# Normalised rows before the transposes, and eight gate blocks emitted before the first short-convolution blocks

## The chip, the cores and the metric

One NeuronCore of a Trainium2 chip runs the whole program. The metric is the device time of one execution in microseconds (us), lower is better. Engines are called as the profile calls them: PE (TensorE), PEld (its weight loads), DVE (VectorE), ACT (ScalarE), POOL (GpSimd), SP (SyncE, which only issues DMAs here).

## What is computed

One encoder layer on x of 1024 positions x 1024 channels, float32:

```
h    = rms_norm(x, g_norm)
proj = h @ w_in                                  # 1024 x 5280
hy_in, z_hy, c_q, c_kv, k_rope, z_attn, gate_hy, gate_attn = split(proj)
v, x1, x2 = split(short_conv(hy_in))             # 3 taps, 512 channels each
spec = rfft(filters from a small sine network)   # does not depend on x
zc = x2 * long_conv(x1 * long_conv(v, spec0), spec1)
u_hy   = (zc * silu(z_hy)) @ w_hy_out
u_attn = (attention(c_q, c_kv, k_rope) * silu(z_attn)) @ w_attn_out
gates  = sigmoid([gate_hy, gate_attn] + b_gate)  # 1024 x 2048
out    = x + (g_hy * u_hy + g_at * u_attn) @ w_out
```

## The kernel before

Every large product is made of three matmuls: each operand is split into a rounded high part and the rest (`split`, L132 to L134: an ACT copy gives the high part, DVE or POOL subtracts it for the low part; `gsplit`, L136 to L138, does the same with a factor per partition), and high x high, low x high and high x low are summed in PSUM.

The stages, in the order in which the program emits them:

- **hT** (`build_hT`, L195 to L231). The eight 128x1024 row tiles of x are transposed on PE into h with channels on partitions, in two halves of 512 positions. For each half: transposes as the tiles land (L204), squares with row sums on DVE or ACT (L210, L212), 1/sqrt by integer guess and three Newton steps on tiny DVE tiles (`rsqrt`), eight matmuls that spread the four columns of row factors over a 128x512 tile R (L218, L220), then for each of eight channel blocks d a DVE multiplication by g_norm and R out of PSUM into `tm` (L230) and a split into hh[d] and hl[d], the low part on POOL for even d. `columns` (L167) transposes the small vectors into per-partition columns.
- **Filter network** (`filter_mlp`): two layers of sines for all positions, mostly DVE instructions of 128x512 (`sin_layer`, L236 to L248). **Tables** (`filter_tables`) and **spectra** (`filter_spectra`, L314 on): four rounds, each of pk matmuls (L333, L334), DVE products and sums, and eight leaves with pu matmuls (L128).
- **First short-conv blocks** (`proj_vx(0)`): four of the 41 projection blocks. A projection block (`proj_block`, L538) loads 128 columns of w_in in two DMAs on SP (L544), splits them (wh on ACT, wl on DVE), and runs 48 matmuls of 128x512 into two PSUM banks pm (L552): 8 d x 3 products x 2 halves of the positions. Four banks are tagged for pm, so two blocks are open at a time. A short-conv block (`short_block`, L573) then copies pm to SBUF (L580, ACT), takes one tap on ACT (L583) and two on DVE (L584, L585); `to_time` transposes the result back and stores it. These blocks and all others keep their SBUF results in one ring of three tiles, tag `ob`.
- **Long convolutions** (`convs(0)`, `proj_vx(1)`, `convs(1)`): chains of leaves, each with pu and pi matmuls. `xz` makes a short-conv block and a SiLU block beside them. The convolutions' pools reuse memory of the filter pools.
- **Latents** (`fill_c`), **q, k, v** (`qkv`), then z blocks (`fill_z`) and the sixteen **gate blocks** (`fill_g`, L662 to L669): a projection block, two ACT sigmoids of 128x512 straight from PSUM into `ob`, one DMA to DRAM issued by ACT. They have no DVE work but the wl split.
- **Attention**, output projections, tail.

The emission order is a priority, not the order of execution: a planner that knows each instruction's inputs, buffers and an estimate of its duration fixes the order on every engine ahead of time, and lets later-emitted work in wherever earlier-emitted work is not ready. Within an engine the fixed order is then kept.

Of the kernel before, what the change touches and what calls it, by code (L numbers as in the profile page):

```python
# [19 lines left out]
P = 128  # L20
# [12 lines left out]
HSPLIT = 3  # L33
CVB, MMB = 2, 4
# [58 lines left out]
class K:  # L93
# [22 lines left out]
    def mm3(self, out, lh, ll, rh, rl, start, stop, after=None):  # L116
        nc = self.nc
        m = nc.tensor.matmul(out, lhsT=lh, rhs=rh, start=start, stop=False)  # L118
        if after is not None:
            self.tc.add_manual_dep(m.ins, after.ins.name, mybir.DependencyInfo(mybir.DependencyClass.NoSync, mybir.DependencyReason.DATA), reason="slack")  # L120
        nc.tensor.matmul(out, lhsT=ll, rhs=rh, start=False, stop=False)  # L121
        nc.tensor.matmul(out, lhsT=lh, rhs=rl, start=False, stop=stop)  # L122

    def mm6(self, out, terms, after=None):

        ops = [(x, t[2]) for t in terms for x in t[:2]] + [(t[0], t[3]) for t in terms]
        for n, (x, y) in enumerate(ops):
            m = self.nc.tensor.matmul(out, lhsT=x, rhs=y, start=n == 0, stop=n == len(ops) - 1)  # L128
            if n == 0 and after is not None:
                self.tc.add_manual_dep(m.ins, after.ins.name, mybir.DependencyInfo(mybir.DependencyClass.NoSync, mybir.DependencyReason.DATA), reason="slack")  # L130

    def split(self, x, hi, lo, eng=None):  # L132
        self.nc.scalar.copy(out=hi, in_=x)  # L133
        (eng or self.nc.vector).tensor_tensor(out=lo, in0=x, in1=hi.bitcast(F32), op=ALU.subtract)  # L134

    def gsplit(self, x, g, hi, lo):  # L136
        self.nc.scalar.activation(out=hi, in_=x, func=AF.Copy, scale=g)
        self.nc.vector.scalar_tensor_tensor(out=lo, in0=x, scalar=g, in1=hi.bitcast(F32), op0=ALU.mult, op1=ALU.subtract)  # L138

# [16 lines left out]
    def setup(self, xp):  # L156
# [7 lines left out]
        self.selr = xp.tile([P, P], F32, tag="selr", name="selr")  # L164
        nc.scalar.dma_start(out=self.selr, in_=a["sel"])

    def columns(self):  # L167
# [16 lines left out]
        self.sel = cp.tile([P, P], F32R, tag="sel", name="sel")  # L184
        nc.scalar.copy(out=self.sel, in_=self.selr)


    def load_x(self, xp, g):
        self.xt = getattr(self, "xt", [])
        for tt in range(4 * g, 4 * g + 4):  # L190
            x = xp.tile([P, D], F32, tag=f"x{tt}", name=self.nm("x"))
            self.nc.sync.dma_start(out=x, in_=self.a["x"][0, tt * P:(tt + 1) * P, :])
            self.xt.append(x)

    def build_hT(self, hp, xp):  # L195
        nc, a = self.nc, self.a
# [3 lines left out]
        xt = self.xt  # L200
        for g in range(2):
            tags = ("mm", "mm", "mm", "mm", "tp", "tp", "cv") if g == 0 else ("tp", "tp", "cv")
            bank = lambda t: self.pp.tile([P, 512], F32, tag=t, bufs={"mm": MMB, "tp": 2, "cv": CVB}[t], name=self.nm("ptx"))
            tr = lambda d, i: nc.tensor.transpose(out=ps[d][:, i * P:(i + 1) * P], in_=xt[4 * g + i][:, d * P:(d + 1) * P], identity=self.ident)  # L204
            ps = {d: bank(t) for d, t in enumerate(tags)}
            for i in range(4):
# [6 lines left out]
                for d in range(len(tags)):  # L213
                    tr(d, i)
            rs = self.rsqrt(xp, ss[:, 4 * g:4 * g + 4], 1.0 / D, [P, 4], "xr")
            pr = self.pp.tile([P, 4, P], F32, tag="cv", bufs=CVB, name=self.nm("prs"))
            for i in range(4):
                nc.tensor.matmul(pr[:, i], lhsT=rs[:, i:i + 1].broadcast_to([P, P]), rhs=self.ident, start=True, stop=True)  # L218
            R = xp.tile([P, 512], F32, tag="R", name=self.nm("R"))
            nc.scalar.copy(out=R, in_=pr.rearrange("p a b -> p (a b)"))  # L220
            if g == 0:
                self.columns()
            sl = slice(g * 512, (g + 1) * 512)
            for d in range(8):
                if d not in ps:
                    ps[d] = bank(("tp", "cv")[d % 2] if g else "tp")
# [1007 lines left out]
```

## Time and profile before

| | us |
|---|---|
| median of 3 runs (lowest to highest) | 1177.83 (1176.38 to 1181.05) |
| the profiled execution | 1176.94 |
| span in its trace | 1174.9 |
| PE busy in the span | 1111.1 |
| DVE busy in the span | 902.8 |
| ACT busy in the span | 585.0 |

The trace covers one execution from its first to its last instruction; 2.0 us of the execution lie outside the span. Matmuls overlap, so the mean duration of one is longer than the distance between two. The granted clock is that of PE: 1.00 is 2.4 GHz, 0.50 is 1.2 GHz, values between are means over a stretch.

### The profile page before, as it was taken

The numbers are of one execution on the slowest core, as the hardware profiler recorded it, in microseconds if no ns is written. First come the engines' busy times: TensorE is split into PE (matmuls) and PEld (weight loads), VectorE is DVE, ScalarE is ACT, GpSimd is POOL, SyncE is SP. The second block draws the span as 40 slices with busy tenths as digits, with TensorE's granted clock in tenths as the row PEclk, the third lists the DMA queues.
The fourth block names the chain that finished last, engine by engine and source line by source line (L and its number), as shares of the span: only waits on it lengthen the run. The fifth ranks groups of instructions, "written<-read, shape, count | busy, mean of one in ns | idle before, by whom it ended". The sixth has DMA issues, their size and how long they took to land.

```text
span 1174.9 us, 15580 instructions
## 1 busy us (share of the span) xinstructions
PE 1111.1 (95%) x5541; PEld 916.1 (78%) x5541; DVE 902.8 (77%) x1629; ACT 585.0 (50%) x1096; POOL 121.2 (10%) x118
## 2 busy tenths in 40 slices
PE   4979989999999999999999999999999999999996
PEld 3757767788888878888887887788888888777875
DVE  5889988898787776877756991388888888668872
ACT  5546454655443523434425742477777777322320
POOL 3200000000000000000000234100000000132253
PEclk7979989999999999999999999999999999999999
DMA  5344445443234344343338458420202010786335
GB/s 190 94 121 147 137 152 197 157 148 89 86 99 121 121 117 126 95 143 90 90 109 264 143 169 297 144 81 2 99 1 90 1 63 2 249 279 206 88 128 179
DMA packets 119221, 150.27 MB, mean 128 GB/s; under 512 B 8548, under 2 KB 82408, under 8 KB 119144
## 3 DMA queue, kind: packets, MB, share of 16 engines
q1 hardware_dynamic: 107832, 122.88, 34.0%
q10 hardware_dynamic: 11312, 26.42, 6.0%
q8 instruction: 43, 0.70, 0.3%
q14 instruction: 34, 0.28, 0.1%
HBM read 101.81 MB, written 47.45 MB: 127 GB/s over the span
## 4 chain that ended last, share of the span: by engine, by line
PE 72%; DVE 12%; DMA 7%; ACT 5%; issue 2%; POOL 1%; SPq 0%; POOLq 0%; DVEq 0%; ACTq 0%
PE pm L552 32%; PE pu L128 6%; PE pt L886 5%; PE pi L128 4%; PE S L118 2%; PE S L121 2%; PE S L122 2%; PE pmo L118 2%; PE pv L898 2%; PE pmo L121 2%; PE pmo L122 2%; PE pv L899 2%; PE po L121 2%; PE po L118 2%; PE po L122 2%
## 5 line engine op out<-in xcount | busy, mean ns | idle before, releaser
L552 PE MATMUL pm<-hh,wh 128*128 128x512 f32 x656 | 212.2, 397 | 6.7 <-DVE sg L626 3.7
L552 PE MATMUL pm<-hl,wh 128*128 128x512 f32 x656 | 210.1, 395 | 0.5 <-POOL hl L134 0.4
L552 PE MATMUL pm<-hh,wl 128*128 128x512 f32 x656 | 209.2, 394 | 0.5 <-DVE wl L134 0.4
L552 PEld LDWEIGHTS pm<-hh,wh 128*128 128x128 f32 x656 | 124.4, 190 | 35.4 <-DVE sg L626 4.9
L133 ACT CAST wh<-wr 128x512 fp32r<-128x512 f32 x98 | 60.5, 620 | 172.5 <-PE pm L552 139.7
L552 PEld LDWEIGHTS pm<-hh,wl 128*128 128x128 f32 x656 | 123.8, 189 | 27.1 <-DVE wl L134 2.1
L552 PEld LDWEIGHTS pm<-hl,wh 128*128 128x128 f32 x656 | 123.9, 190 | 26.6 <-POOL hl L134 1.2
L134 DVE TENSOR_TENSOR wl<-wr,wh 128x512 fp32r<-128x512 f32 x95 | 71.1, 751 | 43.4 <-ACT wh L133 43.0
L134 DVE TENSOR_TENSOR PTl<-pt,PTh 128x512 fp32r<-128x512 f32 x128 | 84.0, 682 | 14.0 <-ACT PTh L133 13.7
L133 ACT CAST PTh<-pt 128x512 fp32r<-128x512 f32 x128 | 72.8, 587 | 43.3 <-PE pt L886 41.5
L871 DVE TENSOR_REDUCE mx<-S 128x1 f32<-128x1024 f32 x64 | 77.8, 1218 | 10.5 <-PE S L122 10.3
L886 PE MATMUL pt<-ident,pr 128*128 128x128 f32 x512 | 75.1, 276 | 1.1 <-ACT pr L873 0.2
L873 ACT ACTIVATE pr<-S,mx 128x1024 f32<-128x1024 f32 x64 | 71.7, 1121 | 5.7 <-DVE mx L871 5.1
L886 PEld LDWEIGHTS pt<-ident,pr 128*128 128x128 f32 x512 | 59.0, 140 | 15.5 <-ACT pr L873 2.9
L898 PE MATMUL pv<-PTh,vc 128*128 128x256 f32 x256 | 69.0, 297 | 0.0
L458 DVE TENSOR_TENSOR t<-pu,kt 128x512 f32<-128x512 f32 x64 | 41.1, 682 | 35.2 <-PE pu L128 34.3
L899 PE MATMUL pv<-PTl,vc 128*128 128x256 f32 x256 | 67.8, 293 | 0.0
L133 ACT CAST rh<-res 128x512 fp32r<-128x512 f32 x64 | 39.3, 618 | 41.8 <-DVE res L366 17.2
L118 PE MATMUL S<-kh,qh 96*128 96x512 f32 x128 | 53.0, 414 | 1.7 <-ACT pr L873 1.6
L121 PE MATMUL S<-kh,ql 96*128 96x512 f32 x128 | 52.5, 410 | 0.0
L898 PEld LDWEIGHTS pv<-PTh,vc 128*128 128x128 f32 x256 | 48.6, 190 | 4.4 <-DVE at L909 1.6
L799 POOL TENSOR_TENSOR k<-k,ry 128x512 f32<-128x512 f32 x8 | 11.6, 1452 | 380.8 <-DVE rv L146 377.4
(289 smaller groups left out, 2469.6 us busy)
## 6 DMA issues: line engine op xcount, KB each, us to landing
wr<-in_w_in_dram SPq DMA_DIRECT2D x82, 256.0 KB, 3.2
wor<-in_w_out_dram SPq DMA_DIRECT2D x36, 256.0 KB, 4.8
dec<-in_dec_dram SPq DMA_DIRECT2D x16, 512.0 KB, 4.2
gT<-ob ACTq DMA_DIRECT2D x16, 512.0 KB, 3.2
gg<-gT SPq DMA_DIRECT2D x16, 512.0 KB, 4.5
kd<-kt ACTq DMA_DIRECT2D x28, 256.0 KB, 2.4
kt<-kd SPq DMA_DIRECT2D x28, 256.0 KB, 2.7
x<-in_x_dram SPq DMA_DIRECT2D x8, 512.0 KB, 6.1
```

The costliest lines, as they stand in the source:

```text
L118: m = nc.tensor.matmul(out, lhsT=lh, rhs=rh, start=start, stop=False)
L121: nc.tensor.matmul(out, lhsT=ll, rhs=rh, start=False, stop=False)
L122: nc.tensor.matmul(out, lhsT=lh, rhs=rl, start=False, stop=stop)
L128: m = self.nc.tensor.matmul(out, lhsT=x, rhs=y, start=n == 0, stop=n == len(ops) - 1)
L133: self.nc.scalar.copy(out=hi, in_=x)
L134: (eng or self.nc.vector).tensor_tensor(out=lo, in0=x, in1=hi.bitcast(F32), op=ALU.subtract)
L552: nc.tensor.matmul(ps[c][0:m], lhsT=w[:, i, 0:m], rhs=h[d][:, c * 512:(c + 1) * 512], start=(d == 0 and f == 0), stop=(d == 7 and f == 2))
L871: nc.vector.tensor_reduce(out=mx, in_=ps, axis=AX.X, op=ALU.max, negate=True)
L873: nc.scalar.activation(out=pr, in_=ps, func=AF.Exp, bias=mx, accum_out=RS[h // 2][:, qb, h % 2:h % 2 + 1])
L886: nc.tensor.transpose(out=pt[:, i], in_=pr[:, kb * P:(kb + 1) * P], identity=self.ident)
L898: nc.tensor.matmul(pv, lhsT=V[h][:, kb], rhs=hi[:, kb], start=(kb == 0), stop=False)
L899: nc.tensor.matmul(pv, lhsT=V[h][:, kb], rhs=lo[:, kb], start=False, stop=(kb == 7))
```

## The change

Rows of x are multiplied by their own factor before they are transposed (tiles xs, DVE), so that squares and factors come first and the eight spreading matmuls, R and `tm` go; g_norm goes into the split, which reads PSUM on both engines. POOL has no part in hT or in z2 any more. The x tiles are issued by SP and ACT in turn, all eight ahead of the filter's loads, and those go to SP. The filter network's first splits are ordered behind the last split of hT's first half on ACT, the cast of `sel` behind the network. The weight tiles wh and wl get four buffers each. Eight of the sixteen gate blocks are emitted behind the filter spectra, ahead of `proj_vx(0)`.

```diff
@@ constants
+GEARLY = 8
...
@@ class K
-    def split(self, x, hi, lo, eng=None):
-        self.nc.scalar.copy(out=hi, in_=x)
+    def behind(self, i, after):
...
+    def split(self, x, hi, lo, eng=None, after=None):
+        self.behind(self.nc.scalar.copy(out=hi, in_=x), after)
         (eng or self.nc.vector).tensor_tensor(out=lo, in0=x, in1=hi.bitcast(F32), op=ALU.subtract)
...
@@ def load_x
-            self.nc.sync.dma_start(out=x, in_=self.a["x"][0, tt * P:(tt + 1) * P, :])
+            (self.nc.sync, self.nc.scalar)[tt % 2].dma_start(out=x, in_=self.a["x"][0, tt * P:(tt + 1) * P, :])
@@ def build_hT
-            ps = {d: bank(t) for d, t in enumerate(tags)}
             for i in range(4):
                 tt = 4 * g + i
...
-                for d in range(len(tags)):
-                    tr(d, i)
-            rs = self.rsqrt(xp, ss[:, 4 * g:4 * g + 4], 1.0 / D, [P, 4], "xr")
-            pr = self.pp.tile([P, 4, P], F32, tag="cv", bufs=CVB, name=self.nm("prs"))
-            for i in range(4):
-                nc.tensor.matmul(pr[:, i], lhsT=rs[:, i:i + 1].broadcast_to([P, P]), rhs=self.ident, start=True, stop=True)
-            R = xp.tile([P, 512], F32, tag="R", name=self.nm("R"))
-            nc.scalar.copy(out=R, in_=pr.rearrange("p a b -> p (a b)"))
             if g == 0:
                 self.columns()
+            rs = self.rsqrt(xp, ss[:, 4 * g:4 * g + 4], 1.0 / D, [P, 4], f"xr{g}")
+            xs = []
+            for i in range(4):
+                x = xp.tile([P, D], F32, tag="xs", bufs=4, name=self.nm("xs"))
+                nc.vector.tensor_scalar(out=x, in0=xt[4 * g + i], scalar1=rs[:, i:i + 1], scalar2=None, op0=ALU.mult)
+                xs.append(x)
...
+            def tr(d, i):
+                nc.tensor.transpose(out=ps[d][:, i * P:(i + 1) * P], in_=xs[i][:, d * P:(d + 1) * P], identity=self.ident)
+
+            n = 7 if g == 0 else 2
+            for d in range(n):
+                ps[d] = bank(tags[d])
+            for i in range(4):
+                for d in range(n):
+                    tr(d, i)
             for d in range(8):
                 if d not in ps:
...
-                t = xp.tile([P, 512], F32, tag="tm", bufs=3, name=self.nm("tm"))
-                nc.vector.scalar_tensor_tensor(out=t, in0=ps[d], scalar=self.gn[:, d:d + 1], in1=R, op0=ALU.mult, op1=ALU.mult)
-                self.split(t, self.hh[d][:, sl], self.hl[d][:, sl], (nc.gpsimd, nc.vector)[d % 2])
+                i = self.gsplit(ps[d], self.gn[:, d:d + 1], self.hh[d][:, sl], self.hl[d][:, sl])
+            self.half0 = getattr(self, "half0", i)
@@ def filter_loads, filter_mlp
+        self.selr = f1.tile([P, P], F32, tag="selr", name="selr")
+        nc.sync.dma_start(out=self.selr, in_=a["sel"])
...
-        nc.scalar.dma_start(out=self.wf1, in_=a["wf1"])
+        nc.sync.dma_start(out=self.wf1, in_=a["wf1"])
...
-        self.split(self.wf1, w1h, w1l)
-        self.split(self.wf2, w2h, w2l)
+        self.split(self.wf1, w1h, w1l, after=self.half0)
+        self.split(self.wf2, w2h, w2l, after=self.half0)
...
-            self.split(z2[:, sl], zh[:, sl], zl[:, sl], nc.gpsimd)
+            self.split(z2[:, sl], zh[:, sl], zl[:, sl], after=self.half0)
@@ def proj_block (the same in proj_rope for wh)
-            wh = wp.tile([P, 4, P], F32R, tag="wh", bufs=3, name=self.nm("wh"))
-            wl = wp.tile([P, 4, P], F32R, tag="wl", bufs=3, name=self.nm("wl"))
+            wh = wp.tile([P, 4, P], F32R, tag="wh", bufs=4, name=self.nm("wh"))
+            wl = wp.tile([P, 4, P], F32R, tag="wl", bufs=4, name=self.nm("wl"))
@@ def hyena_mla_kernel
-                    k.load_x(xp, 0)
                     k.setup(xp)
+                    k.load_x(xp, 0)
+                    k.load_x(xp, 1)
                     k.filter_loads(f1)
-                    k.load_x(xp, 1)
                     k.build_hT(hp, xp)
                     k.filter_mlp(fp, f1)
+                    k.selection()
...
                     with k.pool("fwk") as wk:
                         k.filter_spectra(wk)
+                        for b in range(GEARLY):
+                            k.fill_g(b)
...
-            for b in range(16):
+            for b in range(GEARLY, 16):
                 k.fill_g(b)
```

## Rows read from the trace of the kernel before

**Rows 1.** Page, busy time of each engine (share) and instructions.

```profile
PE 1111.1 (95%) x5541; PEld 916.1 (78%) x5541; DVE 902.8 (77%) x1629; ACT 585.0 (50%) x1096; POOL 121.2 (10%) x118
```

**Rows 2.** Windows, all engines: stretch, its us, busy (instructions) each, PEclk, DMA share, GB/s.

```profile
0.00:25.00 25.00, 9.18 (x41) 7.72 (x41) 11.76 (x27) 12.61 (x25) 7.60 (x12) 0.75 0.64 223
25.00:50.00 25.00, 23.43 (x105) 17.90 (x106) 22.01 (x42) 12.17 (x20) 8.40 (x6) 0.90 0.28 76
50.00:75.00 25.00, 16.46 (x67) 13.03 (x67) 23.69 (x36) 16.19 (x24) 0.13 (x2) 0.78 0.16 47
75.00:100.00 25.00, 25.00 (x127) 21.30 (x126) 21.54 (x37) 10.03 (x18) 0.13 (x2) 0.95 0.68 200
100.00:150.00 50.00, 47.92 (x227) 37.33 (x227) 45.83 (x92) 29.60 (x66) 0.27 (x4) 1.00 0.46 150
150.00:200.00 50.00, 42.64 (x197) 34.60 (x196) 42.42 (x81) 26.51 (x53) 0.13 (x2) 0.90 0.49 158
200.00:250.00 50.00, 48.42 (x228) 39.22 (x227) 45.10 (x82) 29.28 (x58) 0.27 (x4) 1.00 0.52 177
250.00:400.00 150.00, 150.00 (x695) 124.41 (x694) 123.56 (x239) 69.04 (x135) 0.53 (x8) 1.00 0.35 102
400.00:600.00 200.00, 200.00 (x915) 163.67 (x915) 144.12 (x295) 77.99 (x159) 0.00 (x0) 1.00 0.37 110
...
700.00:750.00 50.00, 47.02 (x202) 37.70 (x201) 12.23 (x13) 15.97 (x25) 17.13 (x11) 0.97 0.73 250
```

**Rows 3.** Waits of PE: who waited for whom, us in total, times, longest.

```profile
PE pk L333 <- DVE h L291: 6.5, 1, 6.5
...
PE pu L128 <- ACT rh L133: 4.8, 1, 4.8
```

**Rows 4.** Line L669, the stores of the gate blocks: first and last start.

```profile
L669 ACTq DMA_DIRECT2D gT<-ob x16: 321/326/397, 501.1 to 748.8; - x16
```

**Rows 5.** Timeline, 10 to 28 us: start, us, what, idle before and its releaser.

```profile
10.53 1.23 DVE L210 SCALAR_TENSOR_TENSOR sq<-x 128x1024 f32<-128x1024 f32 x1 [0.48 <-DMA x<-in_x_dram]
...
12.38 2.49 POOL L134 TENSOR_TENSOR zl<-z,zh 128x512 fp32r<-128x512 f32 x2 [9.63 <-ACT zh L133]
12.49 1.18 DVE L150 TENSOR_TENSOR rt<-ry 128x4 f32<-128x4 f32 x1
...
16.10 0.16 DVE L152 SCALAR_TENSOR_TENSOR ry<-rt,ry 128x4 f32<-128x4 f32 x1
...
20.27 1.11 PE L204 MATMUL ptx<-ident,x 128*128 128x128 f32 x4 [0.73 <-ACT cols L172]
...
25.81 0.78 PE L552 MATMUL pm<-hh,wh 128*128 128x512 f32 x1
```

**Rows 6.** Line L242, a DVE operation with one SBUF input: ns min/median/max.

```profile
L242 DVE TENSOR_SCALAR sk<-sx x4: 411/416/429, 46.7 to 61.6; 128x512 f32<-128x512 f32 x4
```

**Rows 7.** Line L138, the low part with a factor, out of PSUM.

```profile
L138 DVE SCALAR_TENSOR_TENSOR ql<-pth,gq,qh x16: 737/737/747, 752.1 to 963.0; 96x512 fp32r<-96x512 f32 x16
```

**Rows 8.** Windows of L552 alone: stretch, us, PE, PEld busy (x), PEclk, DMA, GB/s.

```profile
0.00:50.00 50.00, 17.26 (x59) 11.74 (x60) 0.83 0.46 149
50.00:80.00 30.00, 16.88 (x62) 12.62 (x62) 0.77 0.30 85
80.00:250.00 170.00, 95.41 (x378) 69.30 (x377) 0.97 0.50 164
```

**Rows 9.** Chain of waits, 300 to 345 us: start, us, piece.

```profile
318.39 23.59 PE pm L552 x104
```

**Rows 10.** Groups of DVE, 75 to 250 us: count, busy us, mean ns, idle before.

```profile
L134 DVE TENSOR_TENSOR wl<-wr,wh 128x512 fp32r<-128x512 f32 x16 | 10.9, 678 | 1.8 <-ACT wh L133 1.8
L584 DVE SCALAR_TENSOR_TENSOR acc<-sraw,cols,acc 128x1024 f32<-128x1024 f32 x6 | 7.7, 1276 | 2.5 <-issue 2.2 <-ACT acc L583 0.2
```

**Rows 11.** Line L248, sines on ACT and their table load.

```profile
L248 ACT ACTIVATE sx<-sx x4: 623/630/632, 52.2 to 70.8; 128x512 f32<-128x512 f32 x4
L248 ACT ACT_TABLE_LOAD  x1: 1283/1283/1283, 49.3 to 49.3; - x1
```

More of the change, by code (lines that the diff above doesn't have):

```diff
@@ L118, in mm3 @@
         m = nc.tensor.matmul(out, lhsT=lh, rhs=rh, start=start, stop=False)
-        if after is not None:
-            self.tc.add_manual_dep(m.ins, after.ins.name, mybir.DependencyInfo(mybir.DependencyClass.NoSync, mybir.DependencyReason.DATA), reason="slack")
+        self.behind(m, after)
         nc.tensor.matmul(out, lhsT=ll, rhs=rh, start=False, stop=False)
@@ L128, in mm6 @@
             m = self.nc.tensor.matmul(out, lhsT=x, rhs=y, start=n == 0, stop=n == len(ops) - 1)
-            if n == 0 and after is not None:
-                self.tc.add_manual_dep(m.ins, after.ins.name, mybir.DependencyInfo(mybir.DependencyClass.NoSync, mybir.DependencyReason.DATA), reason="slack")
-    def split(self, x, hi, lo, eng=None):
-        self.nc.scalar.copy(out=hi, in_=x)
+            if n == 0:
+                self.behind(m, after)
+    def behind(self, i, after):
+        if after is not None:
+            self.tc.add_manual_dep(i.ins, after.ins.name, mybir.DependencyInfo(mybir.DependencyClass.NoSync, mybir.DependencyReason.DATA), reason="order")
+    def split(self, x, hi, lo, eng=None, after=None):
+        self.behind(self.nc.scalar.copy(out=hi, in_=x), after)
         (eng or self.nc.vector).tensor_tensor(out=lo, in0=x, in1=hi.bitcast(F32), op=ALU.subtract)
     def gsplit(self, x, g, hi, lo):
-        self.nc.scalar.activation(out=hi, in_=x, func=AF.Copy, scale=g)
+        i = self.nc.scalar.activation(out=hi, in_=x, func=AF.Copy, scale=g)
         self.nc.vector.scalar_tensor_tensor(out=lo, in0=x, scalar=g, in1=hi.bitcast(F32), op0=ALU.mult, op1=ALU.subtract)
+        return i
     def rsqrt(self, pool, ss, inv_n, shape, tag):
@@ L183, in columns, with selection @@
         self.ssc = cp.tile([P, 2, 8], F32, tag="ssc", name="ssc")
-        self.sel = cp.tile([P, P], F32R, tag="sel", name="sel")
-        nc.scalar.copy(out=self.sel, in_=self.selr)
+    def selection(self):
+        self.sel = self.cp.tile([P, P], F32R, tag="sel", name="sel")
+        self.nc.scalar.copy(out=self.sel, in_=self.selr)
     def load_x(self, xp, g):
@@ L200, in build_hT @@
         xt = self.xt
+        bank = lambda t: self.pp.tile([P, 512], F32, tag=t, bufs={"mm": MMB, "tp": 2, "cv": CVB}[t], name=self.nm("ptx"))
         for g in range(2):
-            tags = ("mm", "mm", "mm", "mm", "tp", "tp", "cv") if g == 0 else ("tp", "tp", "cv")
-            bank = lambda t: self.pp.tile([P, 512], F32, tag=t, bufs={"mm": MMB, "tp": 2, "cv": CVB}[t], name=self.nm("ptx"))
-            tr = lambda d, i: nc.tensor.transpose(out=ps[d][:, i * P:(i + 1) * P], in_=xt[4 * g + i][:, d * P:(d + 1) * P], identity=self.ident)
-            ps = {d: bank(t) for d, t in enumerate(tags)}
             for i in range(4):
@@ new lines, in build_hT @@
+            sl = slice(g * 512, (g + 1) * 512)
+            tags = ("mm", "mm", "mm", "mm", "tp", "tp", "cv", "tp") if g == 0 else ("tp", "cv") * 4
+            ps = {}
+            def tr(d, i):
[6 more added lines that the diff above has]
+                    tr(d, i)
@@ L562, in proj_rope @@
         nc.sync.dma_start(out=raw, in_=src[:, :, c0:c0 + 32])
[L563 removed]
+        w = wp.tile([P, 8, 64], F32R, tag="wh", bufs=4, name=self.nm("wh"))
         nc.scalar.copy(out=w[:, :, 0:32], in_=raw)
```

11 lines of the change are left out of this document (4 added, 7 removed).

## The prediction

> **What bounds the kernel now.** I read the busy shares first: PE is busy 95% of the span, DVE 77%, ACT 50% [rows 1]. A kernel in that state can gain in two ways: less PE work, or fewer holes in PE. So the next view is the windows [rows 2], read for two things in each stretch, PE's idle time and its granted clock. From 250 to 600 us PE has no hole and the clock stands at 1.00. Before 250 us it has both: 15.8 us idle in the first 25, 8.5 in 50 to 75 at a mean clock of 0.78, 7.4 in 150 to 200 at 0.90. To put both in one unit I count as lost the idle time plus the busy time multiplied by one minus the clock: 13.4 us for 50 to 100 (8.54 + 3.62 + 0 + 1.25) and 15.3 us for 100 to 250 (2.08 + 7.36 + 4.26 + 1.58). This overstates the clock's part where PE waits anyway, so it is a bound.
>
> Then the waits of PE [rows 3] tell what fills these holes. The longest one, 6.5 us, is the first pk matmul behind DVE's last subtraction of the filter network; another, 4.8 us, is a pu matmul behind a split. Such waits belong to the spectra and would be harmless if PE had something else. It has nothing: the projection blocks that the planner lets in there are short-conv blocks, and each needs DVE work (L584, L585, 1.28 us an instruction [rows 10]) before its ring buffers come free, while DVE is busy 23.7 of 25 us in just that stretch [rows 2]. The blocks that need no DVE but for the two wl splits, the gate blocks, all come after 501 us [rows 4].
>
> Last, the reserve at the other end: from 700 to 750 us PE is 94% busy with DVE at 12.2 of 50 [rows 2]. That stretch is left-over projection work that nothing on DVE waits for. Work that PE does earlier shortens it one for one.
>
> **The change part by part.** The sum is made against the profiled execution, 1176.94 us, of which 1174.9 are the span; it lies 0.9 us under the median of 1177.83.
>
> *Start, hT.* Before: the last of the first four x tiles is squared at 10.53 for 1.23 us; the Newton chain ends at 16.26, two of its tiny instructions taking 1.2 us instead of 0.16 while POOL subtracts zl; spreading, copying and the columns go on to 20.3; the first projection matmul starts at 25.81 [rows 5]. By 50 us 59 of them are done [rows 8]. At full pace one takes 23.59 / 104 = 0.227 us [rows 9].
> After: squares end near 11.8 as now. The chain of eleven instructions at about 0.2 us ends at 14.0, since POOL does nothing then (16.2 if the slow ones stay). Four scalings of 128x1024: a DVE instruction with one SBUF input takes 0.416 us for 512 columns [rows 6] and 0.16 at 4 columns, so 0.66 as an estimate on that line; the upper bound is 1.23, the square of the same shape. That gives 16.6 (to 21.1). The last tile's seven transposes follow, four of them taking 1.11 us at the low clock [rows 5], 2 us: 18.6. Then eight splits at DVE's pace of 0.74 [rows 7]; PE can start with the first, at 19.2, and the half is complete at 25. The second half costs DVE 2.2 + 2.6 + 8 x 0.74, about 37 with its transposes. In the first half two blocks can run on half of their columns, 48 matmuls, until about 38; the remaining 12 us to 50 give 53 more. That is 101 against 59; less 6 small matmuls of the network and some waiting for wl I take 30 more: 30 x 0.227 = 7 us. Bounds: 12 us if nothing waits; with both upper bounds above (16.2, then 1.23 each) hT would be finished near 46, as now, and DVE, which takes over POOL's share, would be later by some 4: so -4.
> Edits that cost nothing: x on two queues (four issues of L192 move from SP to ACT, ahead of z2 and the small loads; 223 GB/s pass in the first 25 us [rows 2], and I take the landing of the first four tiles as unchanged), three small loads leaving ACT's queue for SP's against four x issues coming, the cast of sel. Cover: ACT has 25 us of 50 free there [rows 2]. If the four issues were not hidden, each would put off the first ACT square, some 2 us in all.
>
> *50 to 100 us.* The gate blocks need wl, 2 x 0.68 us of DVE [rows 10], for 10.9 us of PE (48 x 0.227). With them PE runs while DVE makes the sines. They free the ring through ACT and a store alone. Bounds 0 (wl waits behind all of the network) and 13.4. DVE leaves small holes between dependent instructions, into which a planner can put wl, and four buffers allow a block more of lead: I take 9.
> Each gate store is issued by ACT in its own order and waits for the sigmoid before it; behind it stand the casts rh of the spectra. 0.33 us each [rows 4], eight times, moved rather than added.
> Sines and sigmoids now fall into one stretch. There is one table load of 1.28 us ahead of all four sines [rows 11]; interleaved, each sine could need one and each sigmoid after it another: at most 8 x 1.28 = 10 us of ACT, half of them on the network's chain. PE's gate work hides them; without that cover 5 us. The Trainium skill (ScalarE: Activation LUTs, section What ACT_TABLE_LOAD costs) sets a switch at 2.66 us with the drain it adds, and advises finishing one set before the next; by that the chain would be later by an estimated 11 us instead of 5, and the forecast would lose the part of it that is not covered. No row here shows the drain.
>
> *100 to 250 us.* The spectra are bound by DVE (85 to 92% [rows 2]). About half of the short-conv blocks that run here now go later, each taking 2 x 1.28 us of DVE along; eight gate blocks (87 us of PE) come instead. Bounds 0 and 15.3. What the planner's estimates miss stays as holes, so I take 9.
>
> *Later.* The displaced short-conv blocks, about five, bring 13 us of DVE work into 250 to 600, where DVE has 82 us free of 350 [rows 2]: hidden, at a price of 0 to 6 us if it lies on the convolutions' chain; I take 2. The first convolution needs four short-conv blocks, which now come after eight others; PE has work meanwhile. What is late there is covered by the left-over stretch, of which some 40 us are left at 700 (PE works 47 of the 50 us there, with its edges).
>
> Sum: 7 + 9 + 9 - 2 = 23 us. 1176.9 - 23 = 1154, and 0.9 more for the median: **1155**. Best bounds: 12 + 13.4 + 15.3 = 41 us, 1137. Worst: start -4 and later -6, nothing gained: 1188.
>
> **The rivals.**
> *Half of it.* The gate blocks fill the holes of 50 to 100, but the spectra's holes come from buffers and DMA waits that every filler shares, and the start gains little: 3 + 9 + 3 - 2 = 13 us, 1165. For it: the 4.8 us wait falls at a low-activity moment between two rounds, where pm banks may be full. Against it: with fillers of the same machinery PE has no hole from 250 to 600.
> *The holes only move.* PE is fuller before 250, but the fillers are then short at 600 to 750: PE would stand idle in the q, k, v stage. The stretch after 700 holds some 40 us of pure filler, more than the gain, which speaks against it. Time: 1177.
> *DVE bounds the front.* hT now takes DVE 16 x 0.74 + 8 x (0.66 to 1.23) plus z2's two subtractions, against 16 x 0.74 and half of the subtractions before. If wl of the gate blocks is placed behind the network, PE has two open blocks (22 us of matmuls) between 20 us and the first pk matmul and then nothing, as now, and the spectra start later by DVE's extra 4 us; with hT as late as its upper bound (4 more): 1177.8 + 8 = 1186. It decides where fewer than six wl splits stand ahead of the first pk matmul. For it: DVE is the fullest engine there. Against it: the zl contention goes.
> That the gate blocks are not let in at all is excluded by the order: they are the next projection work in priority, and projection blocks already run in these holes.
>
> **How the numbers follow.** Forecast, 1147 to 1160: 0.56; better than that: 0.06; half: 0.17; holes only move: 0.11; DVE bounds the front: 0.10. A measurement of this kernel can tell about 0.5%, 5.9 us, from no change, so the bounds are 1171.9 and 1183.7. Faster: 0.56 + 0.06 + 0.15 of the half case = 0.77; slower 0.09; the same 0.14. The range leaves out most of the better case and the last two cases' upper parts: 1143 to 1176.
>
> **What would show it.** PE's first projection matmul near 19 us and over 85 of them by 50 us; PE over 97% busy at clock 1.00 from 50 to 100; gate stores beginning near 45 us and eight of them before 200; the first leaf of the convolutions starting earlier than now; POOL with no work before 250; a shorter stretch between the last DVE work of q, k, v and the attention. Wrong: a pk wait of PE on DVE that stays, more than three table loads before 100 us on the chain, or new holes of PE between 250 and 700.

## The result, and the profile after

The changed kernel takes 1157.74 us (median of four runs, 1156.19 to 1159.08) where the kernel before takes 1177.11 (four runs, 1174.64 to 1181.05): a ratio of 0.9832 [0.9801, 0.9863]. It is faster, by 19.4 us (1.7%), and lies in the range, 2.7 us above the forecast of 1155. The profiled execution has a span of 1156.9 us against 1174.9, so 18.0 us are to be found in the trace.

The page's busy times after the change, to be held against [rows 1]:

```profile
PE 1098.8 (95%) x5525; PEld 912.7 (79%) x5525; DVE 894.0 (77%) x1631; ACT 589.2 (51%) x1097; POOL 106.7 (9%) x108
```

The shares are the same; what moved is where PE's holes lie. The windows of all engines after, with the columns of [rows 2]:

```profile
0.00:25.00 25.00, 8.99 (x40) 8.08 (x41) 13.51 (x42) 13.50 (x25) 2.09 (x6) 1.00 0.69 244
25.00:50.00 25.00, 24.05 (x122) 19.01 (x121) 24.82 (x42) 20.86 (x30) 0.00 (x0) 1.00 0.31 84
50.00:75.00 25.00, 18.65 (x84) 15.43 (x83) 20.84 (x36) 10.96 (x16) 0.00 (x0) 0.80 0.53 167
75.00:100.00 25.00, 25.00 (x117) 20.62 (x116) 22.07 (x48) 15.02 (x33) 0.00 (x0) 1.00 0.47 160
100.00:150.00 50.00, 50.00 (x254) 42.03 (x253) 40.81 (x82) 24.07 (x50) 0.14 (x2) 1.00 0.57 182
150.00:200.00 50.00, 50.00 (x246) 41.73 (x245) 43.53 (x90) 27.54 (x59) 0.00 (x0) 1.00 0.48 168
200.00:250.00 50.00, 49.32 (x243) 40.87 (x242) 39.83 (x68) 30.68 (x58) 0.53 (x8) 1.00 0.53 159
...
700.00:750.00 50.00, 41.12 (x195) 33.37 (x194) 17.74 (x33) 20.80 (x33) 18.76 (x13) 0.93 0.73 246
```

With the prediction's own unit (idle time plus busy time times one minus the clock), the first 50 us lose 17.0 us where they lost 22.0 in [rows 2], 50 to 100 lose 10.1 (6.35 + 18.65 x 0.20) where it was 13.4, and 100 to 250 lose 0.7 where it was 15.3. That is 5.0 + 3.3 + 14.6 = 22.9 us gained before 250. The 5.0 is the least sure of them: the clock of the first row is no measurement, since this trace has no clock record before 21.6 us (the one of before has none before 9.3), and the windows print 1.00 where there is none. With the lower level taken for that time, which the pace of the transposes bears out (last section), the first 50 us lose an estimated 20.0 where they lost 23.7, and 3.7 + 3.3 + 14.6 = 21.6 are gained. The last line runs the other way: PE stands idle for 8.9 of the 50 us from 700, where it was 3.0.

The first projection matmuls that the gain consists of, counted in the windows of the projection's line alone (L567, before L552):

```profile
0.00:50.00 50.00, 21.72 (x83) 15.11 (x84) 1.00 0.50 164
50.00:80.00 30.00, 19.71 (x74) 14.68 (x73) 0.83 0.58 184
80.00:250.00 170.00, 112.65 (x458) 84.37 (x457) 1.00 0.51 165
```

Against [rows 8] that is 24, 12 and 80 matmuls more, 116 in all, and at 0.227 us [rows 9] 26.3 us of PE work done ahead at 250 us. The lead is still there at the end of the projections: the last one starts at 720.6, before at 747.4, 26.8 us earlier. But the first score matmul starts at 737.1 against 754.8, only 17.7 earlier, and from there to the end it is 419.8 us against 420.1. So about 9 us are lost between the last projection and the first score. The waits of PE say where:

```profile
PE pth L857 <- ACT ob L683: 7.1, 1, 7.1
...
PE pk L348 <- DVE h L306: 5.9, 1, 5.9
```

The second of them is the wait of [rows 3], still there. The first is new. The timeline of ACT around it shows what ACT did meanwhile:

```profile
719.69 1.05 ACT L138 CAST yh<-yr 128x1024 fp32r<-128x1024 f32 x1 [8.47 <-DMA yr<-yT]
721.04 1.04 ACT L138 CAST yh<-yr 128x1024 fp32r<-128x1024 f32 x1 [0.30 <-DMA yr<-yT]
722.31 1.04 ACT L138 CAST yh<-yr 128x1024 fp32r<-128x1024 f32 x1 [0.23 <-DMA yr<-yT]
723.26 1.21 ACT L138 CAST wh<-wr 128x512 fp32r<-128x512 f32 x2
726.47 1.04 ACT L138 CAST yh<-yr 128x1024 fp32r<-128x1024 f32 x1 [2.00 <-DMA yr<-yT]
727.42 1.26 ACT L683 ACTIVATE ob<-pm,cols 128x512 f32<-128x512 f32 x2
```

The last gate sigmoid (L683) frees the PSUM banks that the transposes of q and k (pth) need. Its projection ended at 721.0, but in ACT's order it stands behind four casts of the convolution's output, and each of these waits for its load. The timeline of SP's DMA queue shows when the loads were issued:

```profile
705.53 0.36 SPq L818 DMA_DIRECT2D qd<-q  x1
...
710.00 1.68 SPq L991 DMA_DIRECT2D yr<-yT  x3
...
723.20 0.34 SPq L991 DMA_DIRECT2D yr<-yT  x1
```

The first loads are issued behind the last stores of q and k, at 710.0, and before the change they were issued at 710.5: that end did not move. The data were not what they waited for, since the last store of yT starts at 618.4; issuing the loads earlier was not tried. Before, the same sigmoid started at 747.55, at once after its last projection, because the casts had long been done (the last yh at 725.30). The convolution chain ends where it did (the last pi matmul starts at 595.4, before at 596.8; the last pkv matmul at 686.6, before at 682.3); PE's own work now ends 27 us earlier, ahead of what q, k, v and the loads behind them deliver.

### The profile page after: what moved, and what is told of

Read it like the earlier page. It is cut to its first block, busy times and chain, and to the rows that moved or that the text cites. A ratio compares the mean times of both kernels' runs of the same rounds, so it can differ in the third digit from the quotient of the medians.

```text
span 1156.9 us, 15518 instructions
## 1 busy us (share of the span) xinstructions
PE 1098.8 (95%) x5525; PEld 912.7 (79%) x5525; DVE 894.0 (77%) x1631; ACT 589.2 (51%) x1097; POOL 106.7 (9%) x108
## 4 chain that ended last, share of the span: by engine, by line
PE 77%; DVE 8%; DMA 8%; ACT 4%; issue 2%; POOL 1%; SPq 0%; POOLq 0%; ACTq 0%; DVEq 0%
PE pm L567 35%; PE pu L128 8%; PE pt L901 5%; PE pi L128 4%; PE S L119 2%; PE S L121 2%; PE S L122 2%; PE pv L913 2%; PE pv L914 2%; PE po L122 2%; PE po L121 2%; PE po L119 2%; PE pmo L121 1%; PE pmo L119 1%; ACT pr L888 1%
## 5 line engine op out<-in xcount | busy, mean ns | idle before, releaser
L567 PE MATMUL pm<-hh,wh 128*128 128x512 f32 x656 | 208.8, 394 | 1.4 <-DVE hl L143 0.5
L567 PE MATMUL pm<-hl,wh 128*128 128x512 f32 x656 | 209.4, 394 | 0.0
L567 PE MATMUL pm<-hh,wl 128*128 128x512 f32 x656 | 208.3, 392 | 0.1
L567 PEld LDWEIGHTS pm<-hh,wh 128*128 128x128 f32 x656 | 123.1, 189 | 27.3 <-ACT wh L138 0.7
L567 PEld LDWEIGHTS pm<-hh,wl 128*128 128x128 f32 x656 | 123.4, 189 | 26.0 <-DVE wl L139 0.5
L567 PEld LDWEIGHTS pm<-hl,wh 128*128 128x128 f32 x656 | 123.5, 189 | 25.4
L138 ACT CAST wh<-wr 128x512 fp32r<-128x512 f32 x98 | 60.3, 621 | 152.0 <-PE pm L567 106.9
L138 ACT CAST PTh<-pt 128x512 fp32r<-128x512 f32 x128 | 72.8, 587 | 43.6 <-PE pt L901 41.8
L886 DVE TENSOR_REDUCE mx<-S 128x1 f32<-128x1024 f32 x64 | 77.8, 1218 | 10.5 <-PE S L122 10.1
L139 DVE TENSOR_TENSOR wl<-wr,wh 128x512 fp32r<-128x512 f32 x95 | 66.2, 702 | 16.2 <-ACT wh L138 16.1
L138 ACT CAST rh<-res 128x512 fp32r<-128x512 f32 x64 | 39.5, 619 | 42.8 <-PE pu L128 20.2
L122 PE MATMUL S<-kl,qh 96*128 96x512 f32 x128 | 50.8, 398 | 0.0
```

The lines of the kernel that those rows point to most:

```text
L138: self.behind(self.nc.scalar.copy(out=hi, in_=x), after)
L567: nc.tensor.matmul(ps[c][0:m], lhsT=w[:, i, 0:m], rhs=h[d][:, c * 512:(c + 1) * 512], start=(d == 0 and f == 0), stop=(d == 7 and f == 2))
L886: nc.vector.tensor_reduce(out=mx, in_=ps, axis=AX.X, op=ALU.max, negate=True)
```

## The experiments

Two ends have to meet before attention: PE's queue of projections, and the chain from the first convolution through q, k and v to the casts yh. The theory was that new hT and gate blocks each give a part of the gain and add up, that the wait at 728 is worth its 7 us, and that the hole at 53 us comes from wl on DVE. Each of these three was tried. Ratios are against the kernel before on the same chip, whose medians lie between 1174.8 and 1177.1.

**Without the early gate blocks.**

```diff
-GEARLY = 8
+GEARLY = 0
```

> The changed kernel with no gate block ahead of the first short-conv blocks (all sixteen after the z blocks again); the new hT and all else stay. Theory: the start keeps its 5 us (some 24 more projection matmuls by 50 us), and the holes of PE between 50 and 250 us come back, since the short-conv blocks wait for DVE: 1168 to 1174 us, about 0.993 to 0.997 of the kernel before, PE idle 15 us or more from 50 to 250. Rival (the new hT and the free POOL carry the gain, the gate blocks only move holes): 1160 us, 0.986.

Measured: 1164.9 us, 0.992 [0.9904, 0.9937], better than the theory and short of the rival. The holes do come back: PE is idle for 16.6 us from 50 to 250, with the gate blocks for 7.0. The change without the early blocks, which is the new hT with the edits around it (the order of the splits, the loads, four weight buffers), is worth half of the gain. Below it is called the new hT; of these edits the queues of x and the splits of z2 were tried by themselves, the buffers and the rest were not. The convolutions start earlier than in the changed kernel (first pu matmul of a convolution at 234.7 against 236.2), the last projection starts at 734.3.

**The early gate blocks alone, in the kernel before.**

```diff
+GEARLY = 8
...
+                        for b in range(GEARLY):
+                            k.fill_g(b)
...
-            for b in range(16):
+            for b in range(GEARLY, 16):
```

> The kernel before with nothing changed but eight gate blocks emitted ahead of the first short-conv blocks. Theory: the holes from 50 to 250 us close as in the changed kernel, the start is as before: 1160 to 1166 us, 0.985 to 0.990 of the kernel before. Rival (the new hT carries the gain): 1172 us or more.

Measured: 1174.56 us, 1.0002 [0.9991, 1.0013]: nothing, and the theory of two parts that add falls. The windows show that the gate blocks do what they were meant to do between 100 and 250 us (columns as in [rows 2]):

```profile
100.00:150.00 50.00, 48.73 (x232) 40.03 (x231) 38.27 (x80) 26.64 (x58) 0.00 (x0) 1.00 0.48 161
150.00:200.00 50.00, 49.24 (x248) 40.60 (x247) 40.73 (x80) 23.16 (x49) 0.14 (x2) 1.00 0.54 182
200.00:250.00 50.00, 49.84 (x237) 41.12 (x237) 39.06 (x67) 31.70 (x59) 0.40 (x6) 1.00 0.54 171
```

The last projection starts at 734.9, 12.5 us earlier than before. But the first convolution waits for four short-conv blocks that now stand behind eight others: it starts at 251.4 instead of 246.3, 22.2 us after the last pu matmul of the spectra instead of 15.4, and the chain ends later by more (last pi 612.7 instead of 596.8, last pkv 700.9 instead of 682.3). ACT at the other end, in the timeline of the same run:

```profile
736.05 1.04 ACT L134 CAST yh<-yr 128x1024 fp32r<-128x1024 f32 x1 [10.54 <-DMA yr<-yT]
...
742.65 1.04 ACT L134 CAST yh<-yr 128x1024 fp32r<-128x1024 f32 x1 [1.97 <-DMA yr<-yT]
743.60 1.26 ACT L669 ACTIVATE ob<-pm,cols 128x512 f32<-128x512 f32 x2
```

The last sigmoid again stands behind yh, 8.3 us after the last projection's end, and the first score comes at 753.9, 0.9 earlier than before. With the new hT the chain starts some 12 to 15 us earlier, which is the room that the gate blocks use.

**How many early gate blocks.** Four, twelve and six instead of eight, the constant alone; the diff of the first:

```diff
-GEARLY = 8
+GEARLY = 4
```

> The changed kernel with four gate blocks ahead of the first short-conv blocks instead of eight. Theory: attention's first score matmul starts at the later of two ends, that of PE's projection work, and that of the q, k, v stage plus some 50 us (686.6 and 737.1 in the changed kernel, 700.9 and 753.9 with the gate blocks alone, but 677.2 and 742.4 with none ahead, where PE's work ends last). Eight blocks ahead put off the convolutions, so the second ends last; with four the two are near each other: first scores at 732 to 736, the time 1152 to 1156 us, 0.977 to 0.982 of the kernel before. Rival (each block ahead fills PE further, in proportion): half way between none and eight, first scores near 740, 0.987 to 0.989.

> The changed kernel with twelve gate blocks ahead. Theory: the convolutions, and with them the last pkv matmul, come later again, at 691 us or more; first scores at 741 or more, 1160 to 1166 us, 0.985 to 0.990 of the kernel before. Rival (more blocks ahead, fewer holes): first scores at 737 or earlier, not over 1158 us.

> The changed kernel with six gate blocks ahead. Theory (first scores wait for the later of PE's projection work and the q, k, v stage; the first convolution starts when PE has finished the gate blocks ahead and four short-conv blocks, but not before the spectra let it, at 234 us): the first pu matmul of the convolutions stays at 233 to 237 us, the projection work ends near 726, first scores at 732 to 736, the time 1152 to 1156 us, 0.978 to 0.982 of the kernel before. Rival (what four gain at one end they lose at the other, whatever the number between): 0.983 as with four and eight, first scores at 737 or later.

Measured: four 1156.57 us, 0.9831 [0.9809, 0.9852]; twelve 1188.99, 1.0106 [1.0087, 1.0126]; six 1160.63, 0.9877 [0.9859, 0.9894]. Four is as good as eight, six is 0.5% behind them, just clear of the interval of four, and twelve is slower than no change at all. For four and six I had expected 1152 to 1156 us and first scores from 732 to 736: both came out above. Why six is behind four is not shown; the spans of the three traces (1157.9, 1157.7, 1156.9) do not tell them apart. The starts of five steps in the traces, in us, with two runs of below:

| run | first convolution pu | last pi | last pkv | last projection | first score |
|---|---|---|---|---|---|
| before | 246.3 | 596.8 | 682.3 | 747.4 | 754.8 |
| gate blocks alone | 251.4 | 612.7 | 700.9 | 734.9 | 753.9 |
| new hT, none early | 234.7 | 588.4 | 677.2 | 734.3 | 742.4 |
| new hT, four | 233.8 | 585.6 | 674.0 | 730.9 | 739.0 |
| new hT, six | 232.5 | 590.7 | 678.4 | 728.8 | 739.9 |
| the change, eight | 236.2 | 595.4 | 686.6 | 720.6 | 737.1 |
| new hT, twelve | 279.5 | 637.9 | 724.7 | 661.8 | 757.2 |
| casts behind, eight | 234.6 | 594.4 | 683.9 | 717.9 | 729.1 |
| three ahead of the network, six | 254.8 | 609.1 | 696.9 | 721.6 | 741.3 |

Read the last two columns together. Where the chain is early (before, none, four) the first score follows the last projection by 7.4 to 8.1 us. From four on, the more gate blocks are drawn ahead, the earlier the projections end and the later the chain: from the last projection to the first score it is 11 us with six, 16.5 with eight, 95 with twelve. From none to four the chain does not get later. With twelve PE ran out of projections at 661.8 and waited for the data of q, as the waits of PE in that run show:

```profile
PE pth L857 <- DMA qr<-qd: 27.5, 1, 27.5
```

My expectation for twelve had the direction right and the size far too small. What sets the chain's start stands in the traces too. With none, four and six the first convolution follows the last pu matmul of the spectra by 14.5 to 16.4 us, as before (15.4): the spectra set it, and the gate blocks cost the chain nothing. With eight it is 23.3 us and with twelve 67.7. The first transposes of the short-conv blocks start at 134.8, 171.7, 209.2 and 247.9 with four, six, eight and twelve, and the spectra are done near 212 with eight and with twelve: there the short-conv blocks set it. From eight to twelve the start moves by 43.3 us, which is the time of four gate blocks on PE (4 x 10.9). With four the last projection sets the first score, with eight the chain does, and 739.0 and 737.1 lie 2 us apart.

**The yh casts behind the last sigmoid.** An order is written between the last gate sigmoid and the casts that stood in front of it.

```diff
-            nc.scalar.activation(out=ob[:, sl], in_=ps[c], func=AF.Sigmoid, bias=self.bg[:, b:b + 1])
+            self.lastg = nc.scalar.activation(out=ob[:, sl], in_=ps[c], func=AF.Sigmoid, bias=self.bg[:, b:b + 1])
...
-            self.split(y, self.yh[i], self.yl[i], nc.gpsimd)
+            self.split(y, self.yh[i], self.yl[i], nc.gpsimd, after=self.lastg)
```

> The changed kernel with the four casts of the convolution result (yh, on ACT) ordered behind the last sigmoid of the last gate block. Theory: in the changed kernel PE stands idle 7.1 us ahead of attention's first transposes because that sigmoid, whose matmuls end at 721 us, stands on ACT behind casts that wait for DMAs; with the order turned the wait falls under 2 us and the time by 4 to 6: 1152 to 1154 us, 0.978 to 0.980 of the kernel before. Rival (attention's loads or the first output projection, late by the same, hold PE there): the wait moves to another line and the time stays within 1 us of 1157.7.

Measured: 1164.91 us, 0.9918 [0.9903, 0.9933]. A miss: the last projection ended at 714.2, but the sigmoid came 9 us behind it, since the next waiting casts took the place. The timeline of ACT in this run:

```profile
718.21 1.37 ACT L138 CAST wh<-wr 128x512 fp32r<-128x512 f32 x2 [13.80 <-DMA wr<-in_w_hy_out_dram]
722.97 0.62 ACT L138 CAST wh<-wr 128x512 fp32r<-128x512 f32 x1 [3.39 <-DMA wr<-in_w_hy_out_dram]
723.49 1.26 ACT L683 ACTIVATE ob<-pm,cols 128x512 f32<-128x512 f32 x2
```

PE's wait became 10.0 us, and the first score is at 737.1 as in the changed kernel.

**Those weight casts behind it as well** (the edit below beside that of above), and the same with four early blocks (GEARLY = 4).

```diff
-            self.split(r, wh, wl, nc.gpsimd if self.mb == 1 else nc.vector)
+            self.split(r, wh, wl, nc.gpsimd if self.mb == 1 else nc.vector, after=self.lastg if d < HSPLIT and g0 == 0 else None)
```

> The changed kernel with the yh casts and the casts of the first three blocks of the convolution branch's output weights all ordered behind the last sigmoid of the gate blocks on ACT. In the run with the yh casts alone, those weight casts took their place: the last projection matmul ended at 714 us, the sigmoid waited until 723.5 for a cast that waits for a DMA. Theory: now the sigmoid follows the matmuls, PE's wait ahead of attention's transposes falls below 3 us, first scores at 730 to 734; the time 1151 to 1156 us, unless the output blocks that now come later lengthen the last stage (some 180 us from the last scores to the end, 184.8 in that run). Rival (attention's loads hold PE): the wait stays at 5 us or more.

> Four gate blocks ahead, and the same order of the casts. Theory: with four ahead PE's projection work ends near 730 us, little before attention could start, so the order of the casts has less to give: within 3 us of the run with four blocks ahead alone. Rival: it adds its whole 5 us, 1147 to 1150 us.

Measured: 1157.94 us, 0.9848 [0.982, 0.9877], and with four 1171.31, 0.995 [0.9929, 0.9972]. The first of them removes the wait on the sigmoid. PE's waits in that run have two shorter ones in its place:

```profile
PE pth L857 <- DVE ql L143: 3.7, 1, 3.7
PE S L119 <- ACT kh L142: 3.5, 1, 3.5
```

The first score is at 729.1, 8.0 earlier than in the changed kernel, and the time stays the same, just above the 1151 to 1156 expected; the exception that the expectation names, a longer last stage, is what came. Where the 8 us went is in the windows of the output projection's matmuls (pmo, TensorE alone: us, busy, instructions, clock), cut at the first score, the start of the last score and the end. The changed kernel, then this run:

```profile
0.00:737.10 737.10, 6.05 (x19) 0.98 0.46 143
737.10:976.90 239.80, 14.79 (x48) 1.00 0.15 48
976.90:1156.90 180.00, 76.14 (x318) 0.97 0.57 184
```

```profile
0.00:729.10 729.10, 0.00 (x0) 0.99 0.45 143
729.10:971.10 242.00, 11.47 (x35) 0.99 0.14 46
971.10:1159.90 188.80, 82.92 (x349) 0.98 0.56 184
```

In the changed kernel 19 of these matmuls run ahead of the scores, and 48 more run beside them. They do not stand in the 7.1 us, in which PE is idle, but behind it (729.8 to 737.1), between the transposes of q and those of k. With the casts pushed back none is ready there, PE waits for ql and kh instead, 35 run beside the scores, and 31 more are left for the last stage, which takes 188.8 us instead of 180.0. So the casts that delayed the sigmoid also made work ready that must be done anyway; pushing them back took the wait and that work away together. The sizes carry some noise: the traced execution of this run lies 4.0 us above its median, that of the changed kernel 1.3. The run with four missed its expectation (within 3 us of four alone) by far, 14.7 us above it, by the same path: its trace has the first score at 740.7 (739.0 with four alone), 241.8 us for the scores (239.8) and 188.2 for the last stage (179.1). The count of 19 also stands in the traces of before, of the gate blocks alone, and with none, four and six; it is 0 with twelve and in the next run, and wherever it is smaller the last stage is longer: 185.1 with the yh casts alone behind the sigmoid (12 ahead), 188.8 and 188.2 with the weight casts too, 186.5 with twelve blocks, against 177.8 to 180.2.

**Three early blocks emitted ahead of the filter network**, six in all: the hole at 53 us.

```diff
-GEARLY = 8
+GEARLY = 6
...
+                    for b in range(3):
+                        k.fill_g(b)
...
-                        for b in range(GEARLY):
+                        for b in range(3, GEARLY):
```

> Six gate blocks ahead, the first three of them emitted before the filter network instead of behind the spectra. With wl on POOL the third block's weights were there by 32 us and the hole of PE at 53 to 59 us stayed: its wh casts stand on ACT behind the sines and the casts of h, at 62 us. Theory: emitted earlier, these casts come before the sines, PE's wait for the first pk matmul falls below 2 us, the clock stays at 1.00 through 50 to 75, and some 25 more projection matmuls are done by 80 us (157 in the changed kernel); the network is later by 1 to 3 us; the time is 2 to 6 us under that with six ahead. Rival: the blocks delay the network on DVE by more than they fill, the first convolution starts 4 us or more later, and the time is the same or above.

Measured: 1176.71 us, 1.0012 [1.0002, 1.0022]. The hole is gone: PE is busy for 25.00 of 25 us from 50 and again from 75, at clock 1.00, and no wait of pk is left among PE's longest. It gains nothing, for the network pays: the first pk matmul starts at 82.8 instead of 59.3 and the first convolution at 254.8 instead of 232.5 (both against six). The end is the one of above, in ACT's timeline,

```profile
729.76 1.04 ACT L138 CAST yh<-yr 128x1024 fp32r<-128x1024 f32 x1 [17.56 <-DMA yr<-yT]
730.71 0.68 ACT L683 ACTIVATE ob<-pm,cols 128x512 f32<-128x512 f32 x1
```

with the last projection done at 722.0; and none of the output matmuls ahead of the scores, so that the last stage takes 187.5. This is the most telling run: PE has 54 more projection matmuls behind it at 250 us than with six (613 against 559) and the kernel is 16 us slower. Here the spectra set the start of the convolutions again, 14.3 us behind their last pu matmul at 240.5.

**wl of the first three gate blocks on POOL**, to free DVE for that hole.

```diff
-        ps = self.proj_block(3232 + b * P, P)
+        ps = self.proj_block(3232 + b * P, P, self.nc.gpsimd if b < 3 else None)
```

> The changed kernel with the low parts wl of the first three gate blocks made by POOL instead of DVE. Theory: PE is dry from 53 to 59 us and then slow until 66 because the third block's wl (and the weight loads that wait for earlier ones) stand behind the filter network on DVE; with POOL making them the hole shrinks below 2 us and PE has done some 25 more projection matmuls by 80 us; the time falls by 2 to 5 us, less what the end has no room for. Rival (POOL's reads slow DVE in the network by as much, 1.2 us instead of 0.2 or 0.7 an instruction, as in the Newton chain of the kernel before): the first pk matmul starts 3 us or more later than 59.2 and the time does not fall.

Measured: 1158.51 us, 0.9865 [0.985, 0.9879]. The hole stays, the wait of pk is 7.3 us. So wl on DVE was not what kept PE short of work at 53 us. POOL itself waits for the third block's wh, from 28.5 to 62.6 us. The timeline of ACT in the changed kernel shows where wh stands:

```profile
53.10 0.69 ACT L683 ACTIVATE ob<-pm,cols 128x512 f32<-128x512 f32 x1 [1.85 <-PE pm L567]
53.81 1.28 ACT L261 ACT_TABLE_LOAD   x1
55.58 1.15 ACT L261 ACTIVATE sx<-sx 128x512 f32<-128x512 f32 x2 [0.49 <-DVE sx L260]
56.64 2.52 ACT L305 CAST h<-sx 64x512 fp32r<-64x512 f32 x4
59.18 1.28 ACT L683 ACT_TABLE_LOAD   x1
60.48 0.69 ACT L683 ACTIVATE ob<-pm,cols 128x512 f32<-128x512 f32 x1
61.06 0.61 ACT L138 CAST wh<-wr 128x512 fp32r<-128x512 f32 x1
```

The next block's wh cast stands in ACT's order behind the sines, the casts of h and a sigmoid. Only four wl splits (18.07, 18.75, 37.30, 46.74) lie ahead of the first pk matmul at 59.19, and the fifth, at 61.70, waits for ACT. That the cast alone, moved ahead of the sines, would close the hole was not tried; the run above moved whole blocks.

**The splits of z2 and of the network's weights as before**: zl on POOL, none of them ordered behind the first half of hT.

```diff
-            self.split(z2[:, sl], zh[:, sl], zl[:, sl], after=self.half0)
+            self.split(z2[:, sl], zh[:, sl], zl[:, sl], nc.gpsimd)
```

> The changed kernel with the split of z2 (and of the network's first weights) as before: low part on POOL, not ordered behind hT's first half. Theory: POOL's reads meet the second Newton chain, whose tiny DVE instructions take up to 1.2 us instead of 0.16, and hT's second half is later by 1 to 3 us; the time is above that of the changed kernel by 0 to 3 us (0.983 to 0.986 of the kernel before). Rival (the contention was a main part of what the new hT gains): 5 us or more.

Measured: 1160.97 us, 0.9878 [0.9861, 0.9895], just outside what was expected; the intervals of this run and of the changed kernel overlap by a hair (0.9861 to 0.9863). In the trace the first split of hT starts at 23.2 instead of 21.7, the last at 38.7 instead of 35.8, and the first score is 3.0 us later (740.1). So engine and order together are worth an estimated 3 us.

**All of x on SP's queue.**

```diff
-            (self.nc.sync, self.nc.scalar)[tt % 2].dma_start(out=x, in_=self.a["x"][0, tt * P:(tt + 1) * P, :])
+            self.nc.sync.dma_start(out=x, in_=self.a["x"][0, tt * P:(tt + 1) * P, :])
```

> The changed kernel with all eight x tiles issued by SP. Theory: the landing is bound by the transfers, not by the issues, so the first scaling starts within 1 us of 15.1 and the time is within 2 us of the changed kernel's, 0.982 to 0.985 of the kernel before. Rival (one queue issues too slowly): the first scaling 2 us later or more.

Measured: 1159.35 us, 0.9865 [0.9842, 0.9888], not told apart from the changed kernel. On one queue the first scaling starts 2.5 us earlier (12.6 instead of 15.1), where I had expected it within 1 us. But the first casts of weights stand behind the casts of h on ACT (21.8 instead of 16.9), and the first projection starts at 22.5 in both. At 100 us 202 projection matmuls are done, with two queues 200; the first scores stand at 736.1 and 737.1.

No kernel tried beats the changed one beyond its interval; four early blocks tie with it.

## Why the prediction was right, and where its steps were not

*Start, 7 us.* Right in kind, 3.7 to 5.0 by lost time and 24 x 0.227 = 5.4 by matmuls (30 were forecast). The chain of small instructions (twelve, I counted eleven) runs without the slow ones of [rows 5]; its end and what follows in the timeline after:

```profile
14.94 0.16 DVE L158 SCALAR_TENSOR_TENSOR ry<-rt,ry 128x4 f32<-128x4 f32 x1
...
15.14 2.74 DVE L223 TENSOR_SCALAR xs<-x,ry 128x1024 f32<-128x1024 f32 x4
...
15.95 6.01 PE L230 MATMUL ptx<-ident,xs 128*128 128x128 f32 x28 [8.63 <-DVE xs L223]
...
20.94 3.58 ACT L142 ACTIVATE hh<-ptx,cols 128x512 fp32r<-128x512 f32 x6 [2.58 <-PE ptx L230]
21.66 2.73 DVE L143 SCALAR_TENSOR_TENSOR hl<-ptx,cols,hh 128x512 fp32r<-128x512 f32 x4 [0.58 <-ACT hh L142]
```

A scaling takes 0.69 us (2.74 for four; I took 0.66) and the chain ends at 15.1 (14.0), since the squares end at 12.7 (11.8). The step that failed is the first projection at 19.2: it came at 22.5. I let the last tile's seven transposes, 2 us, follow the scalings, and the scalings are done at 17.9. But the 28 transposes take 6.01 us on PE, 0.21 each, and end only at 22.0; no bank is complete before the last tile's. Twelve transposes of the second half, from 28.98 on, take 1.47 us, 0.12 each: the first ones ran at the lower clock. hT was complete near 36.5, as forecast (37).

*50 to 100 us, 9 us.* Mis-sized: 3.3. The step "four buffers allow a block more of lead" failed, and the condition that I gave to a rival, fewer than six wl splits ahead of the first pk matmul, was met: there are four. The hole stayed, but the spectra did not start later, as that rival had it (their first pu on rl at 84.2, before at 98.4), so its 1186 did not follow. The limit was not wl on DVE; it was, as far as the timelines show, ACT's order, and the run with three blocks ahead of the network shows that the hole must not be bought with the network's time. The prediction names a pk wait that stays as a sign of being wrong, and for this stage it was one.

*100 to 250 us, 9 us.* Mis-sized the other way: 14.6 of at most 15.3. I kept 6 us for holes that the planner would leave; it left 0.7. In sum the three stages came out at 21.6 to 22.9 against 25, but by luck: the errors of the last two cancel.

*Later, -2.* This step failed: of the 21.6 to 22.9 us gained before 250, 18.0 are left in the span, so the term is nearer -4 to -5. The prediction said that a stretch of some 40 us of left-over projections would cover what is late on the convolution's chain, and that work done earlier shortens it one for one. PE's projections ended 26.8 us earlier, and by that the stretch was used up: of it 17.7 us reached the first score, some 9 were lost, 7.1 of them behind ACT's queue. The sign "new holes of PE between 250 and 700" came true in part: PE is idle for 5.7 us from 600 to 700, before for 2.6. The rival "the holes only move" named this stretch, and twelve early blocks and the three ahead of the network show it in full. The prediction also took the gate blocks and the new hT as separate terms of a sum. They are not: 0.992 for hT, 1.000 for the gate blocks, 0.983 for both.

*Table loads.* Seven instead of four; the two switches on the network's chain cost less than the 5 us feared. ACT's rows above show one: the casts of h end at 59.16, the load starts at 59.18 and the sigmoid at 60.48, so a switch costs ACT 1.32 us with all its edges. The Trainium skill (ScalarE: Activation LUTs, section What ACT_TABLE_LOAD costs) gives 2.66 us with a drain; the trace shows no drain, and the measured 1.32 decides. In front of the first sines the load delays the chain by 0.8 us (it ends at 44.20, the sine's input was ready at 43.39). In front of the last sines the load ends at 55.09, and the sine waits for DVE until 55.58: the load was hidden.

*What the parts are worth* is shown: the new hT with its side edits by the run without early blocks, the interplay by the gate blocks alone, what the wait before attention is worth (nothing, once the work that goes with it is counted) by the casts moved behind the sigmoid. That early blocks delay the chain because four short-conv blocks stand behind them is read from the traces with four to twelve: up to six the spectra hide it (232.5 to 234.7), at eight some 8 us of it show, and from eight to twelve all of it. What lengthens the chain between the first pu and the last pi at eight was not tried by itself and stays open.

## What to carry to other kernels

Before filling an engine's holes with work from the end, look which of two things the end waits for, that engine's own queue or a chain beside it: filler pays until both end together, and beyond that each block drawn ahead delays the chain (four and eight blocks tie here, twelve cost 2.8% against eight). Ask also what starts the chain: early blocks were free as long as the spectra ended last, and cost their whole PE time after that. Before a wait is removed by moving what causes it, count the work that this made ready: here 19 matmuls ahead of the scores went with it, and the last stage took them back. And in an in-order queue look at what stands ahead of the instruction that frees the buffers, above all casts that wait for a DMA.

## What the runs showed that was not expected

- DVE's smallest operations grow while POOL subtracts. With zl on POOL again (17.02 to 20.25) two Newton operations of 128x4 took 1.27 and 1.24 us, and 0.17 without, as in [rows 5]. The run with wl on POOL shows it again (1.26 and 1.20 us while POOL subtracts from 17.50 to 20.02).
- TensorE's clock at the start cannot be read from the first row of the windows. After the change the first clock record of the trace begins at 21.6 us, at 1.00 (2.4 GHz). Until then the first 28 transposes of 128x128 go at 0.21 us each (6.01 us), where twelve from 28.98 on take 0.12 each (1.47 us), so the clock was at its lower level, 1.2 GHz, and rose while PE did nothing but transposes. After the hole from 53.3 to 59.2 us it stood at the lower level, 1.2 GHz: the mean of 50 to 75 us is 0.80, and a pair of pm matmuls takes 1.22 us at 61.72 and again 0.63 at 66.07.
